# RMSNorm and matrix product: TensorE's program as a loop of sixteen tiles, and one store in 126 and 2 rows

## Chip, cores, metric

The kernel runs on one core of a Trainium2 chip. The metric is the device time of one execution in microseconds (us). A profiled execution also leaves a trace; its span runs from the first to the last instruction of the program, and all moments below are counted from the span's start.

A core has five engines, each with its own instruction stream: TensorE (PE; its weight loads are PEld), VectorE (DVE), ScalarE (ACT), GpSimd (POOL) and SyncE (SP). They meet only at semaphores. Sixteen DMA engines move data between the main memory and the on-chip memory; in this kernel nearly all transfers are issued by SyncE.

## The reference

```python
batch, seq, dim, out_dim = 16, 1024, 512, 768
def reference(x, gamma, weight, eps):
    rms = np.sqrt(np.mean(x ** 2, axis=-1, keepdims=True) + eps)
    x_norm = x / rms * gamma
    return np.matmul(x_norm, weight).astype(np.float32)
```

Inputs and output are float32. Seen as rows, x is 16384 x 512 and the output 16384 x 768.

## The kernel before

**Tiles.** The rows are cut into `NT` = 128 tiles of 128 rows; two tiles make a pair j (`NP` = 64). gamma is multiplied into the weights once, and the weights are kept as bfloat16 (`w_bf`, four blocks of 128 features). The division by the root mean square is left to the end: it scales each row of the product.

**Stages of a tile.** SyncE loads x, mostly sixteen or eight tiles at a time, into one of two buffers `xt`. GpSimd casts it to bfloat16 (`cast`, into `xb`). TensorE turns 128 x 128 blocks of 32-bit words, which hold two bfloat16 each (`transpose_word`, into the PSUM banks `tp`), and VectorE copies them out (`evac`, into `xT`). For the last four tiles of every sixteen, from tile 28 on, the turning is done by VectorE itself, in sixteen small moves (`cast_quad`, `move`, from `xq` into `xTq`; there are two buffers `xTq`). ScalarE squares and sums x for the norms (`square`, `root`), VectorE takes the reciprocal. Then TensorE does four steps of a weight load (`hold`) and two products, 512 and 256 columns wide (`matmuls`), into one of three accumulators `ops`; they are taken in turn, so that tile i uses the one of tile i-3. `finish_tile` scales the product into `ot`: ScalarE for even tiles, VectorE for odd ones. When a group of tiles is complete, SyncE stores it (`store`): eight tiles a store in the middle, at the end stores of 4, 4, 4, 2 and 2 tiles.

**Order.** Nothing is scheduled by a planner. The loop over j at the end of the kernel writes down every operation with the cells that it reads and writes (`order.add`), and `Order.emit` works out which semaphores each must wait for and issues all of them, unrolled, engine by engine in the order written. The transposes for pair j+2 are woven between the products of pair j by `feeder`. Each engine has one semaphore that counts up over the whole program (`done`), and an operation waits for a value of it. The last copy of a group waits for the copy before it (`before` in `finish_tile`), so that the store waits for one engine alone. SyncE's queue is in order: a store that waits holds back the loads behind it. The last store stands apart, after the final waits of the others.

Of the kernel before, what the change touches and what calls it, by code (L numbers as in the profile page):

```python
# [11 lines left out]
F32 = mybir.dt.float32  # L12
BF16 = mybir.dt.bfloat16
# [7 lines left out]
class Order:  # L21
# [1 line left out]

    def __init__(self, tc):  # L30
        self.tc, self.ops = tc, []

    def add(self, proc, engine, issue, reads=(), writes=()):
        self.ops.append((proc, engine, issue, list(reads), list(writes)))

    def transfer(self, engine, issue, reads=(), writes=()):
# [1 line left out]

    def emit(self):
        nc = self.tc.nc  # L40
        streams = {id(e): n for n, e in enumerate((nc.tensor, nc.vector, nc.scalar, nc.gpsimd, nc.sync))}
        writer, readers = {}, {}
        known = [dict() for _ in streams]
        clocks, needs, place, slot_of, slots = [], [], [], {}, []
        count = [0] * len(streams)
        for n, (proc, engine, _, reads, writes) in enumerate(self.ops):
            at = streams[id(engine)]
            if proc is None:
                me, turn = ("transfer", n), 1
            else:  # L50
                count[at] += 1
                me, turn = at, count[at]
            written = {writer[cell] for cell in reads + writes if cell in writer}
            read = {d for cell in writes for d in readers.get(cell, ())}
            need = []
            for d in sorted(written | read, reverse=True):
                who, when = place[d]
                if who == me and (engine is nc.tensor or d not in written):
                    continue
                if known[at].get(who, 0) < when:  # L60
                    need.append(d)
                    for k, v in clocks[d].items():
                        known[at][k] = max(known[at].get(k, 0), v)
            if proc is None:
                free = [k for k, d in enumerate(slots) if known[at].get(("transfer", d), 0)]
                if free:
                    slots[free[0]] = n
                else:
                    slots.append(n)
                slot_of[n] = ("slot", slots.index(n))  # L70
            clock = dict(known[at])
            clock[me] = turn
            place.append((me, turn))
            clocks.append(clock)
            needs.append(need)
            for cell in reads:
                readers.setdefault(cell, []).append(n)
            for cell in writes:
                writer[cell], readers[cell] = n, []
        awaited = {d for need in needs for d in need}  # L80
        seen = {who for clock in known for who in clock}
        last = [n for n, (me, _) in enumerate(place) if me not in seen and not isinstance(me, int)]
        sems, marks, done = {}, {}, {}
        for n in range(len(self.ops)):
            me = slot_of.get(n, place[n][0])
            if n in slot_of or n in awaited:
                if me not in sems:
                    sems[me] = self.tc.alloc_semaphore(f"done{len(sems)}")
                done[me] = done.get(me, 0) + (16 if n in slot_of else 1)
                marks[n] = (sems[me], done[me])  # L90
        for n, (proc, engine, issue, _, _) in enumerate(self.ops[:-1]):
            for d in needs[n]:
                engine.wait_ge(*marks[d])  # L93
            ins = issue()
            if n in marks:
                ins.then_inc(marks[n][0], 16 if n in slot_of else 1)
        return [marks[n] for n in last if n < len(self.ops) - 1], self.ops[-1][2]


@with_exitstack  # L100
def kernel(
# [9 lines left out]
    PE, DVE, ACT, POOL, SP = nc.tensor, nc.vector, nc.scalar, nc.gpsimd, nc.sync  # L111
    order = Order(tc)

    def run(engine, issue, reads=(), writes=()):
        order.add(1, engine, issue, reads, writes)

    x = x.flatten_outer_dims()
    out = out.flatten_outer_dims()
# [37 lines left out]
    jk = [sb(f"jk{n}", [P, D], BF16) for n in range(2)]  # L156
    xT = [sb(f"xT{n}", [P, 2, 2, P, 2], BF16) for n in range(4)]
    xq = [sb(f"xq{n}", [P, 4, D], BF16) for n in range(2)]
    xTq = [sb(f"xTq{n}", [P, 4, 2, P, 2], BF16) for n in range(2)]
    ot = [sb(f"ot{n}", [P, OG, O], F32) for n in range(3)]  # L160
    ssq = sb("ssq", [P, NT], F32)
    rms = sb("rms", [P, NT], F32)
    rstd = sb("rstd", [P, NT], F32)
# [70 lines left out]
    def evac(j, t=0, n=2):  # L234
        b = bank(j, t)
        src = tp[b].rearrange("p t h m -> p t (h m)").bitcast(BF16)
        dst = xT[j % 4].rearrange("p t h m c -> p t (h m c)")
        run(DVE, lambda: DVE.tensor_copy(out=dst[:, t:t + n, :], in_=src[:, t:t + n, :]),  # L238
            [("tp", b)], cells("xT", j % 4, t, n))
        for a in range(t, t + n):  # L240
            xT_of[2 * j + a] = (xT[j % 4][:, a], ("xT", j % 4, a))

    def transpose_tile(i):
        for h in range(2):
# [11 lines left out]
    def cast_quad(q):  # L256
        src, of = x_of(4 * q, 4)
        s = 4 * q // XG % 2
        run(POOL, lambda: POOL.tensor_copy(out=xq[s], in_=src), of, [("xq", s)])  # L259
        for t in range(4):  # L260
            xT_of[4 * q + t] = (xTq[s][:, t], ("xTq", s))
        words = xq[s].rearrange("p t d -> p (t d)").bitcast(F32).rearrange("p (a w) -> p a w", w=P)
        turned = xTq[s].rearrange("p t h m c -> p (t h m c)").bitcast(F32).rearrange("p (a m) -> p a m", m=P)
        for tokens in range(0, P, B):
            for features in range(0, P, B):
                quad_moves.append((turned[features:features + B, :, tokens:tokens + B],
                                   words[tokens:tokens + B, :, features:features + B], s))

    def move(dst, src, s):
        run(DVE, lambda: DVE.transpose(out=dst, in_=src), [("xq", s)], [("xTq", s)])  # L270

    def move_quad(n):
        for _ in range(min(n, len(quad_moves))):
# [5 lines left out]
        else:  # L279
            run(DVE, lambda: DVE.tensor_single_scalar(out=dst, in_=src, scalar=r, op=mybir.AluOpType.mult), reads, writes)  # L280

    turns = iter(range(NT + 1))

    def accumulator():
        return next(turns) % 3

    def store(i):
        first, n = o_first[i], o_size[i]
        s = first // OG % 3
        if i == first + n - 1:  # L290
            src = ot[s][:, first % OG:first % OG + n, :]
            order.transfer(SP, lambda: SP.dma_start(out=rows(out, first, n), in_=src), reads=cells("ot", s, first % OG, n))  # L292

    def hold(lhsT, cell):
        run(PE, lambda: PE.ldweights(lhsT), [cell])  # L295
# [1 line left out]
    def product(dst, lhsT, rhs, start, stop, reads, writes):  # L297

        run(PE, lambda: PE.add_instruction(mybir.InstMatmult(  # L299
            name=nc.get_next_instruction_name(), engine=mybir.EngineType.PE,  # L300
            ins=[PE.lower_ap(rhs), PE.lower_ap(lhsT)], outs=[PE.lower_ap(dst)],
            start_tensor_calc=start, stop_tensor_calc=stop, tile_size=(P, P), tile_position=(0, 0), ldweights=False)),
            reads, writes)

    def matmuls(i, a, ks, feed=None):
        block, cell = xT_of[i]
        for k in ks:
            lhsT = block[:, k // 2, :, k % 2]
# [4 lines left out]
            if feed:  # L313
                feed()

    def finish_tile(i, a, engine):
        s = i // OG % 3

        before = [("ot", s, i % OG - 1)] if i == o_first[i] + o_size[i] - 1 else []
        scale(engine, ot[s][:, i % OG, :], ops[a][:, :O], rstd[:, i:i + 1],  # L320
              [("ops", a, 0), ("ops", a, 1), ("rstd", i)] + before, [("ot", s, i % OG)])
        store(i)

    def feeder(pairs, gaps, alone=False):
        queue = [(j, t, h) for j in pairs for t in range(2) for h in range(2)]
# [17 lines left out]
    def load_weights(h):  # L343
# [10 lines left out]
    run(POOL, lambda: POOL.memset(ident_f, 0.0), [], ["ident"])  # L354
    run(POOL, lambda: POOL.affine_select(out=ident_f, in_=ident_f, compare_op=mybir.AluOpType.not_equal, fill=1.0, base=0,
                                         pattern=[[-1, P]], channel_multiplier=1), ["ident"], ["ident"])
    spare = accumulator()

    def warm_up(n):
        hold(warm[:, :P], "warm")  # L360
        for _ in range(n):
            product(ops[spare][:, :WIDE], warm[:, :P], warm, True, True, ["warm"], [("ops", spare, 0)])

    def weights(k, engine, lo=0, hi=O):
        halves = [half for half in range(2) if lo <= half * WIDE < hi]
# [19 lines left out]
    weights(0, DVE, 0, WIDE)  # L385
    weights(0, DVE, WIDE, O)
    weights(1, ACT)
    acc = [accumulator() for _ in range(2)]
    for i in range(2):
        matmuls(i, acc[i], [0, 1])  # L390
    weights(2, DVE)
    weights(3, ACT)
    norms(2, 2)
    cast(4, 2)
    matmuls(0, acc[0], [2, 3])
    finish_tile(0, acc[0], ACT)
    matmuls(1, acc[1], [2, 3], feeder([1], [2, 2], alone=True))
    finish_tile(1, acc[1], DVE)
    cast(6, 2)


# [2 lines left out]
    for j in range(1, NP):  # L404
# [15 lines left out]
        if j < 3:  # L420
            feed = feeder([j + 1], mid if j == 1 else one, alone=j == 1)
        elif j == 3:
            feed = feeder([4, 5], both)
        elif j + 2 < NP and quad_of(j + 2) is None:
            feed = feeder([j + 2], two)
        else:
            feed = None
        for i, engine in ((2 * j, ACT), (2 * j + 1, DVE)):
            a = accumulator()
            matmuls(i, a, range(K), feed)  # L430
            finish_tile(i, a, engine)


    with tc.tile_critical():  # L434
# [45 lines left out]
```

## Time and profile before

| | |
|---|---|
| Time, median of 3 runs | 209.25 us (208.79, 209.25, 209.55) |
| Profiled execution, span | 207.5 us |
| Instructions | 2761 |
| PE busy | 193.3 us, 93% of the span (1212 instructions) |
| PEld busy | 72.6 us, 35% (717) |
| DVE busy | 149.3 us, 72% (255) |
| ACT busy | 144.5 us, 70% (343) |
| POOL busy | 59.8 us, 29% (34) |
| DMA | 85.62 MB, mean 413 GB/s; the data queue q1 takes 97.3% of 16 engines' span |
| Instruction fetches | q8: 7 packets, 0.11 MB; q14: 5 packets, 0.04 MB |

How to read it: a busy time is the time in which the engine had an instruction in work, and an engine that is busy for most of the span need not be what sets its end. In the page's line of slices the span is cut into 40 equal parts, and a digit is the busy share of one part in tenths. "Idle before" is the time for which an engine had nothing to do before an instruction, and the name behind the arrow is what ended it. A queue q in the DMA list is a ring of transfers: q1 carries the data, q8 and q14 carry instructions for the engines, and q10 the load of gamma. A packet is one piece of a transfer moved by one DMA engine.

### The profile page before, as it was taken

How to read it: one execution, taken by the hardware profiler on the slowest of the kernel's cores; microseconds unless marked ns; L12 is line 12 of the kernel's file. 1: busy time of each engine (PE TensorE's matmuls, PEld its weight loads, DVE VectorE, ACT ScalarE, POOL GpSimd, SP SyncE). 2: the span in 40 equal slices, each digit the busy share in tenths (PEclk: the TensorE clock that was granted, in tenths of full speed). 3: DMA queues.
4: the chain of work that ended last, by engine and by line, in shares of the span. 5: the costliest groups of instructions: out<-in, count | busy, mean ns of one | idle time of the engine just before them, and what ended most of it. 6: DMA issues, size and time to landing. Idle time of an engine off the chain costs nothing.

```text
span 207.5 us, 2761 instructions
## 1 busy us (share of the span) xinstructions
PE 193.3 (93%) x1212; PEld 72.6 (35%) x717; DVE 149.3 (72%) x255; ACT 144.5 (70%) x343; POOL 59.8 (29%) x34
## 2 busy tenths in 40 slices
PE   7779999999999999998999999999999999999940
PEld 1233434433443334342333333443334334433210
DVE  0446556999579966999379984999579984999530
ACT  4698897868777596763977877687867787683310
POOL 2156733009400291003900570006700175000000
PEclk9999999999999999999999999999999999999996
DMA  6999999999999999999999999999999999998993
GB/s 225 403 441 436 388 405 456 455 388 422 436 445 442 395 425 448 429 411 431 434 407 436 437 428 434 418 428 437 417 426 426 433 442 425 426 436 381 407 404 139
DMA packets 5632, 85.62 MB, mean 413 GB/s; under 512 B 626, under 2 KB 628, under 8 KB 1780
## 3 DMA queue, kind: packets, MB, share of 16 engines
q1 hardware_dynamic: 5616, 85.46, 97.3%
q8 instruction: 7, 0.11, 0.2%
q14 instruction: 5, 0.04, 0.0%
q10 hardware_dynamic: 4, 0.00, 0.0%
HBM read 35.13 MB, written 50.33 MB: 412 GB/s over the span
## 4 chain that ended last, share of the span: by engine, by line
PE 71%; DMA 16%; DVE 5%; issue 2%; SPq 1%; ACT 1%; POOL 1%; ACTq 0%
PE ps L299 62%; DMA xt<-in_x_dram 16%; PE ps L229 8%; DVE ot L280 2%; DVE xTq L270 2%; DVE xT L238 1%; SPq L344 1%; POOL xb L187 1%; ACT jk L195 0%; SPq L176 0%; ACT ot L278 0%; SPq L292 0%; DVE rstd L202 0%; SPq L475 0%; ACTq L93 0%
## 5 line engine op out<-in xcount | busy, mean ns | idle before, releaser
L299 PE MATMUL ps<-w_bf,xT 128*128 128x256 bf16 (+1 forms) x783 | 145.0, 325 | 3.4 <-ACT ot L278 1.3
L278 ACT ACTIVATE ot<-ps,rstd 128x768 f32<-128x768 f32 x64 | 57.4, 898 | 42.4 <-PE ps L299 40.5
L195 ACT ACTIVATE jk<-xt 128x512 bf16<-128x512 f32 x128 | 78.8, 619 | 8.3 <-DMA xt<-in_x_dram 8.2
L187 POOL CAST xb<-xt 128x2048 bf16<-128x2048 f32 (+3 forms) x21 | 46.3, 2218 | 113.2 <-DMA xt<-in_x_dram 111.4
L280 DVE TENSOR_SCALAR ot<-ps,rstd 128x768 f32<-128x768 f32 x64 | 64.8, 1013 | 9.9 <-PE ps L299 9.2
L295 PEld LDWEIGHTS <-xT 128*128 128x128 bf16 x400 | 39.3, 98 | 61.2 <-issue 53.2
L229 PE MATMUL ps<-ident_f,xb 128*128 128x128 f32 x200 | 54.4, 277 | 0.9 <-POOL xb L187 0.9
L238 DVE COPY xT<-ps 128x1024 bf16<-128x1024 bf16 (+1 forms) x53 | 34.5, 653 | 24.5 <-PE ps L229 22.8
L270 DVE STREAM_TRANSPOSE xTq<-xq 32x256 f32<-32x256 f32 x112 | 48.7, 435 | 3.4
L229 PEld LDWEIGHTS ps<-ident_f,xb 128*128 128x128 f32 x200 | 28.3, 143 | 46.5 <-issue 42.9
L299 PE MATMUL ps<-w_bf,xTq 128*128 128x256 bf16 (+1 forms) x217 | 41.8, 324 | 0.4
L195 ACT ACTIVATION_READ_ACCUMULATOR jk<-xt 128x1 f32 x128 | 24.3, 190 | 0.0
L295 PEld LDWEIGHTS <-xTq 128*128 128x128 bf16 x112 | 11.0, 98 | 14.5 <-issue 14.5
L259 POOL CAST xq<-xt 128x2048 bf16<-128x2048 f32 x7 | 13.3, 1893 | 0.0
L202 DVE RECIPROCAL rstd<-rms 128x8 f32<-128x8 f32 (+3 forms) x20 | 3.8, 192 | 7.9 <-ACT rms L200 7.7
L200 ACT ACTIVATE rms<-ssq,eps_sb 128x8 f32<-128x8 f32 (+3 forms) x20 | 6.0, 300 | 0.6
L299 PE MATMUL ps<-warm 128*128 128x512 bf16 x10 | 4.4, 582 | 1.4 <-DVE eps_sb L353 1.4
L278 ACT ACTIVATE w_bf<-w_f,g_sb 128x768 bf16<-128x768 f32 x2 | 1.9, 936 | 1.7 <-DMA w_f<-in_weight_dram 1.7
L376 DVE COPY g_sb<-ps 128x4 f32<-128x4 f32 x1 | 0.2, 163 | 3.2 <-PE ps L370 3.2
L340 ACT ACT_TABLE_LOAD x1 | 1.3, 1283 | 1.5 <-SPq L434 1.5
L280 DVE TENSOR_SCALAR w_bf<-w_f,g_sb 128x512 bf16<-128x512 f32 (+2 forms) x3 | 1.4, 481 | 1.1 <-DMA w_f<-in_weight_dram 1.1
L370 PEld LDWEIGHTS ps<-ident_f,g_row 2*128 2x128 f32 x2 | 0.3, 200 | 2.6 <-issue 2.6
(10 smaller groups left out, 2.0 us busy)
## 6 DMA issues: line engine op xcount, KB each, us to landing
out_dram<-ot SPq DMA_DIRECT2D x13, 3072.0 KB, 16.6
xt<-in_x_dram SPq DMA_DIRECT2D x9, 2048.0 KB, 21.1
xt<-in_x_dram SPq DMA_DIRECT2D x3, 4096.0 KB, 22.2
out_dram<-ot SPq DMA_DIRECT2D x4, 1536.0 KB, 11.3
out_dram<-ot SPq DMA_DIRECT2D x3, 768.0 KB, 7.0
w_f<-in_weight_dram SPq DMA_DIRECT2D x2, 768.0 KB, 5.8
xt<-in_x_dram SPq DMA_DIRECT2D x2, 512.0 KB, 5.2
xt<-in_x_dram SPq DMA_DIRECT2D x1, 1024.0 KB, 9.0
```

What stands on the lines that cost most here:

```text
L187: run(POOL, lambda: POOL.tensor_copy(out=xb[s][:, i % 8:i % 8 + n, :], in_=src), of, cells("xb", s, i % 8, n))
L195: run(ACT, lambda: ACT.activation(out=jk[j], in_=src[:, 0, :], func=AF.Square, accum_out=ssq[:, i:i + 1]), of, [("jk", j), ("ssq", i)])
L200: run(ACT, lambda: ACT.activation(out=rms[:, s], in_=ssq[:, s], func=AF.Sqrt, scale=1.0 / D, bias=eps_sb), [("ssq", t) for t in range(i, i ...
L202: run(DVE, lambda: DVE.reciprocal(out=rstd[:, s], in_=rms[:, s]), [("rms", i)], [("rstd", t) for t in range(i, i + n)])
L229: run(PE, lambda: PE.transpose(out=tp[b][:, t, h, :], in_=words[:, lo:lo + P], identity=ident_f), cells("xb", s, j % 4 * 2 + t) + ["ident" ...
L238: run(DVE, lambda: DVE.tensor_copy(out=dst[:, t:t + n, :], in_=src[:, t:t + n, :]), [("tp", b)], cells("xT", j % 4, t, n))
L259: run(POOL, lambda: POOL.tensor_copy(out=xq[s], in_=src), of, [("xq", s)])
L270: run(DVE, lambda: DVE.transpose(out=dst, in_=src), [("xq", s)], [("xTq", s)])
L278: run(ACT, lambda: ACT.mul(out=dst, in_=src, mul=r), reads, writes)
L280: run(DVE, lambda: DVE.tensor_single_scalar(out=dst, in_=src, scalar=r, op=mybir.AluOpType.mult), reads, writes)
L295: run(PE, lambda: PE.ldweights(lhsT), [cell])
L299: run(PE, lambda: PE.add_instruction(mybir.InstMatmult(name=nc.get_next_instruction_name(), engine=mybir.EngineType.PE, ins=[PE.lower_ap(r ...
```

## The change

TensorE's operations for the pairs 6 to 61 (tiles 12 to 123) are no longer issued one by one. `Order.add` notes for each of them its turn (eight pairs, sixteen tiles) and half-turn, and `emit` issues one turn's operations inside a hardware loop on TensorE that runs seven times, its head aligned to a block of instructions. What comes before stays ahead of the loop, and tiles 124 to 127 stay behind it. The other engines' streams stay unrolled.

For the loop each turn must be the same. So the accumulator of a tile follows from its place among sixteen (`accumulator(i)`), there is one buffer `xTq`, which pairs 6 and 7 use too, and the loop has semaphores of its own, one for each engine and half-turn (`own`). VectorE, ScalarE and GpSimd count them up when they finish an operation that the loop waits for, and a later product of the loop takes the whole count off again. Such an operation no longer counts up the engine's common semaphore; whoever else waits for it waits for the engine's next operation that does (`shared`). For that, ScalarE gets a small write to `told` after the last but one tile of a store, and VectorE's copy of the last tile waits for it.

The store of tiles 124 and 125 is issued as two transfers, of 126 rows and of 2.

```diff
     def add(self, proc, engine, issue, reads=(), writes=()):
+        if self.turn is not None and engine is self.tc.nc.tensor:
+            self.body.setdefault(self.turn, []).append((len(self.ops), self.half))
         self.ops.append((proc, engine, issue, list(reads), list(writes)))
...
                 if who == me and (engine is nc.tensor or d not in written):
                     continue
+                if n in spot:
+                    direct.setdefault(n, {}).setdefault(who, d)
...
-        awaited = {d for need in needs for d in need}
+        turns = sorted(self.body)
+        size = len(self.body[turns[0]])
...
+        waits = [sorted({place[d][0] for t in turns for d in needs[self.body[t][q][0]]}) for q in range(size)]
...
+        def shared(d):
+            if d not in events:
+                return d
+            return next(e for e in order[place[d][0]] if e > d and e not in events)
...
+        for (who, half), sem in own.items():
+            final = max(q for q, w in values if w == who and self.body[turns[0]][q][1] == half)
+            q = next(q for q in range(final + 1, size) if q not in flags and q not in taken and self.ops[self.body[turns[0]][q][0]][0] == "product")
+            taken[q] = (sem, -counts[who, half])
+
+        def give(n):
+            _, engine, issue, _, _ = self.ops[n]
             for d in needs[n]:
-                engine.wait_ge(*marks[d])
+                engine.wait_ge(*marks[shared(d)])
             ins = issue()
             if n in marks:
                 ins.then_inc(marks[n][0], 16 if n in slot_of else 1)
+            elif n in events:
+                ins.then_inc(own[place[n][0], events[n][1]], 1)
+
+        behind = max(spot)
+        late = [n for n in outer if n > behind and self.ops[n][1] is nc.tensor]
+        for n in outer:
+            if n < len(self.ops) - 1 and n not in late:
+                give(n)
+        with nc.Fori(0, len(turns), engines=[mybir.EngineType.PE], head_slot={mybir.EngineType.PE: 0}):
+            for q, (n, half) in enumerate(self.body[turns[0]]):
+                for who in waits[q]:
+                    nc.tensor.wait_ge(own[who, half], values[q, who])
+                ins = self.ops[n][2]()
+                if n in marks:
+                    ins.then_inc(marks[n][0], 1)
+                elif q in taken:
+                    ins.then_inc(*taken[q])
+        for n in late:
+            give(n)
...
-    xTq = [sb(f"xTq{n}", [P, 4, 2, P, 2], BF16) for n in range(2)]
+    xTq = sb("xTq", [P, 4, 2, P, 2], BF16)
     ot = [sb(f"ot{n}", [P, OG, O], F32) for n in range(3)]
+    told = sb("told", [P, 1], F32)
...
+        if j in (6, 7):
+            block, to = xTq[:, 2 * (j - 6):2 * (j - 5)], ["xTq"] * 2
+        else:
+            block, to = xT[j % 4], cells("xT", j % 4, 0, 2)
...
-    turns = iter(range(NT + 1))
-
-    def accumulator():
-        return next(turns) % 3
+    def accumulator(i):
+        return (2, 0, 1, 2, 0, 1, 0, 2, 0, 1, 2, 0, 1, 2, 0, 1)[(i - 12) % 16] if i >= 12 else (i + 2) % 3
...
-            order.transfer(SP, lambda: SP.dma_start(out=rows(out, first, n), in_=src), reads=cells("ot", s, first % OG, n))
+            for lo, hi in ((0, P - 2), (P - 2, P)) if first == NT - 4 else ((0, P),):
+                part = rows(out, first, n)[lo:hi], src[lo:hi]
+                order.transfer(SP, lambda part=part: SP.dma_start(out=part[0], in_=part[1]), reads=cells("ot", s, first % OG, n))
...
-        before = [("ot", s, i % OG - 1)] if i == o_first[i] + o_size[i] - 1 else []
+        ends = i == o_first[i] + o_size[i] - 1 and i > o_first[i]
+        before = [("told", i - 1)] if ends else []
...
         store(i)
+        if engine is ACT and i + 1 == o_first[i] + o_size[i] - 1:
+            run(ACT, lambda: ACT.mul(out=told, in_=eps_sb, mul=1.0), ["eps"], ["told", ("told", i)])
...
+        order.turn, order.half = ((j - 6) // 8, (j - 6) % 8 // 4) if 6 <= j < NP - 2 else (None, 0)
```

## The prediction

> **What bounds the kernel now.** I read the page's slices first, then busy time by stretch, then the chain of waits, and last the records of single DMA packets, which the trace keeps. The page:
>
> ```profile
> PE   7779999999999999998999999999999999999940
> PEclk9999999999999999999999999999999999999996
> DMA  6999999999999999999999999999999999998993
> ...
> q8 instruction: 7, 0.11, 0.2%
> ```
>
> TensorE and the 16 DMA engines are both full from the third slice to the last but two. Busy time cut at the same point of three sixteen-tile turns, then the rest (stretch, length, PE, PEld, DVE, ACT, POOL, clock, DMA share, GB/s):
>
> ```profile
> 118.35:141.77 23.42, 23.26 (x151) 8.88 (x88) 19.07 (x33) 17.57 (x43) 6.46 (x4) 1.00 1.00 427
> 141.77:165.19 23.42, 23.26 (x151) 8.88 (x88) 19.07 (x33) 17.32 (x42) 6.12 (x3) 1.00 1.00 427
> 165.19:188.61 23.42, 23.26 (x151) 8.88 (x88) 19.07 (x33) 17.57 (x42) 7.33 (x3) 1.00 1.00 429
> 188.61:199.38 10.77, 10.67 (x66) 3.13 (x32) 6.78 (x11) 3.60 (x4) 0.00 (x0) 1.00 0.93 395
> 199.38:207.54 8.16, 0.00 (x0) 0.00 (x0) 1.01 (x1) 0.00 (x0) 0.00 (x0) 0.79 0.57 235
> ```
>
> A turn takes 23.42 us each time, with TensorE busy 23.26 of it: no gap can be taken from TensorE there, and any gap put in is added. But what ends last is not TensorE (199.3 us). The tail by microsecond:
>
> ```profile
> 202.00:203.00 1.00, 0.00 (x0) 0.00 (x0) 0.00 (x0) 0.00 (x0) 0.00 (x0) 1.00 0.99 412
> 203.00:204.00 1.00, 0.00 (x0) 0.00 (x0) 0.00 (x0) 0.00 (x0) 0.00 (x0) 1.00 0.71 289
> 204.00:205.00 1.00, 0.00 (x0) 0.00 (x0) 0.00 (x0) 0.00 (x0) 0.00 (x0) 0.58 0.24 98
> 205.00:206.00 1.00, 0.00 (x0) 0.00 (x0) 0.00 (x0) 0.00 (x0) 0.00 (x0) 0.50 0.12 49
> ```
>
> The reader is to see the share fall in steps: 0.24 of 16 engines is about four, 0.12 about two. The packet records say it exactly. Each transfer ends with one 4-byte completion on each engine; those of the last store come at 203.60 to 203.93 us on ten engines, at 204.06, 204.44, 205.01, 205.54, 205.59 on five, and at 206.29 on the last. So one engine ends 2.7 us behind the pack, and the span closes 1.24 us after it (207.54). Followed back, packet by packet, the late engine is never idle, while the pack waits for stores between 190 and 200 us (about 2 us in all).
>
> One stall of TensorE is also caused by late loads; ScalarE waited for x, and TensorE for ScalarE:
>
> ```profile
> 96.83 0.63 ACT L195 ACTIVATE jk<-xt 128x512 bf16<-128x512 f32 x1 [3.59 <-DMA xt<-in_x_dram]
> ...
> 98.07 0.88 ACT L278 ACTIVATE ot<-ps,rstd 128x768 f32<-128x768 f32 x1
> 99.00 1.46 PE L299 MATMUL ps<-w_bf,xT 128*128 128x512 bf16 x8 [1.28 <-ACT ot L278]
> ```
>
> **The fetches.** TensorE's 1741 instructions become 449, of which 216 are the body, turned seven times for tiles 12 to 123. Before, q8 makes seven fetches of 16,384 bytes, 23 to 27 us apart. Their packets take 0.89 to 0.98 us, and six times the data packet right behind takes 1.28 to 1.40 us where such a packet has a median of 0.91: about 1.3 us of one engine's time for a fetch. The front, the body (aligned to 256 instructions) and the rest fill three blocks, so I take one fetch to stay and six to go: 6 x 1.3 / 16 = 0.49 us less for an engine on average. By phase the fetches at 50 and 76 us fell on different engines, so they don't pile up. For the latest engine the bounds are 0 (its packets show no fetch after 43 us) and 1.3 (the one at 27 us looks to be its own). I take the mean share, 0.49, since which engine is latest varies.
>
> **The split store.** Tiles 124 and 125 went out as 8 packets of 6,144 bytes on each engine, 0.234 us a packet (1.87 us). The 2-row load of gamma shows what two rows do: q10 has four packets, two of data and two completions, so two engines. 126 rows show nowhere. Bounds: spread like 128 rows, at most 8 an engine, no change; or all on one engine, 126 x 0.234 = 29.5 us. The largest number up to 16 that divides 126 is 14; nearest to the 16 by 8 of the rows seen, I take 14 engines with 9 rows (2.11 us, +0.23), two with none (-1.87), and two with a tenth row (+0.47). If the latest engine is one of the relieved, it ends at 204.4, and the next, 205.59 + 0.23 = 205.82, sets the end: -0.47. If not, +0.23 or +0.47. I take the first. [...]
>
> [...]
>
> **The back edge.** Nothing in the trace is a branch of TensorE. Sequencer records of four engines at the start show compare-and-branch rows of 33 to 47 ns, with the next instruction 0.15 to 0.29 us after their start. Bounds for each of six edges: 0, and a whole fetch, 0.91 for the packet in front plus 0.98 = 1.9 us. I take 0, because work is queued: the body's last wait is for ScalarE's copy of the tile three before. In the turn that ends at tile 91 that copy ran from 143.44 to 144.34 us; the copy of tile 90 began at 146.03, so with tile 91 (4 x 0.325 us) TensorE was supplied until 147.3, 2.9 us later. If that cover is gone: 6 x 0.29 = 1.7 us. Even that is not on the path that ends last, for the pack may slip 2.7 us before it passes the late engine.
>
> [...]
>
> **Accumulators.** Three stay, but two of every sixteen tiles (16m+2 and 16m+4) now wait for the tile two before, not three. ScalarE copies that one in 0.90 us, starting when its tile ends; the tile between, with two transposes, takes 4 x 0.325 + 2 x 0.109 = 1.52. Margin 0.6 us. ScalarE sat 0.92 us idle before each of these copies; late copies (72.6, 98.1) are of tiles 40 and 56, which keep distance three. Cost 0; without the cover up to 14 x 0.9 = 12.6 us.
>
> **The rest.** ScalarE gains 20 tiny writes to `told`, one for each store of more than one tile; the nearest row is the root:
>
> ```profile
> L200 ACT ACTIVATE rms<-ssq,eps_sb 128x2 f32<-128x2 f32 x5 | 1.5, 296 | 0.2
> ```
>
> 0.30 us, inside that 0.92 of idle time; behind it only squares are queued. VectorE's copy of a group's last tile now waits for it; for tile 127 that is 198.97 + 0.30 = 199.27 against a start at 199.38. Cost 0, at most 0.1. Fifteen stores now wait for VectorE's next move (0.44 us) after the copy, and with them the loads behind on SyncE's queue; the DMA share of 0.99 to 1.00 there means a backlog hides it; bare, 15 x 0.44 = 6.6 us. SyncE issues one DMA more (0.33 us, after 197.8), free before the last issue at 200.69. One `xTq` instead of two: the moves follow the copy of tile 16m+15 on VectorE anyway, 0.
>
> **The sum.** -0.49 (fetches) -0.47 (split store) + 0 + 0 = -0.96 us on the profiled execution of 207.54: 206.6. The median of the runs, 209.25, lies 1.7 above that execution, which I carry along: 208.3.
>
> **Rivals.**
> 1. The late engine is neither relieved nor freed of a fetch: 209.25 + 0.23 = 209.5. For it: its chain shows no later fetch, and 14 of 16 engines get more. Against: the delays recur at large loads on few engines.
> 2. All lateness goes: the end is the pack's with ten rows, 203.60 + 0.47 = 204.07 against 206.29, -2.2: 207.0. For it: the six late engines hold all the loss. Against: loads were slow without any fetch.
> 3. Slower: each back edge refetches its block and TensorE's queue doesn't cover it. 6 x 1.9 = 11.4, less the 2.7 of slack: +8.7, 218. It decides from 0.45 us an edge (2.7 / 6). For: nothing in the trace shows how deep that queue is. Against: the 2.9 us and the one-block body.
> 4. 126 rows on few engines, or one uncovered wait above: 210 and more.
>
> **How the numbers follow.** Forecast 0.50, its own range 207.7 to 208.8; rival 1 0.17, rival 2 0.10, rival 3 0.14, rival 4 0.09. Under about 0.3% (0.63 us) a measurement of this kernel can't tell a change from none. Faster: 0.43 of the forecast and rival 2, 0.53; same: 0.07 and rival 1, 0.24; slower: rivals 3 and 4, 0.23. The range: 206.9 holds rival 2, 210.0 rival 1 with its +0.47 and some bare waits; the far rivals stay out.
>
> **What would show it.** q8 with one or two packets; TensorE at 23.42 us a turn with no idle time at the edge; the last microseconds of the DMA shares steeper, the last completion near 205.3; the store of 126 rows in nine packets an engine on 14 engines. Wrong, if turns grow, if instruction packets stay at seven, or if the last engine still ends 2.5 us behind the pack.

## The result, and the profile after

The changed kernel takes 211.28 us (median of 4 runs, 210.84 to 211.93), the kernel before beside it 209.4 us (4 runs, 208.79 to 210.05). The ratio is 1.0105, with a 95% interval of 1.0082 to 1.0127: slower by about 2 us, where 208.3 us was forecast and 210.0 was the upper end of the range.

The profiled execution took 210.84 us; its page (span, slices, DMA queues):

```profile
span 209.0 us, 2823 instructions
...
PE   7789999999999999998999999999999999999900
PEclk9999999999999999999999999999999999999995
DMA  6999999999999899999999999999999999999991
...
q8 instruction: 3, 0.05, 0.1%
```

TensorE's line now ends in two zeros where it ended in 4 and 0: TensorE is done earlier (198.7 us in the trace, 199.3 before), and the span is 1.5 us longer all the same. Three turns of the loop and the rest, cut at the back edges (stretch, length, then busy time of PE, PEld, DVE, ACT and POOL, clock, DMA share, GB/s):

```profile
120.36:143.78 23.42, 23.42 (x153) 8.88 (x88) 19.08 (x33) 17.75 (x45) 6.75 (x3) 1.00 1.00 427
143.78:167.20 23.42, 23.42 (x153) 8.88 (x88) 19.08 (x33) 17.76 (x45) 6.47 (x4) 1.00 1.01 431
167.20:190.62 23.42, 23.42 (x153) 8.88 (x88) 19.07 (x33) 16.45 (x41) 5.17 (x3) 1.00 1.00 427
190.62:198.72 8.10, 8.10 (x50) 2.35 (x24) 4.28 (x6) 2.98 (x6) 0.00 (x0) 1.00 0.95 395
```

A turn has its 23.42 us, with no idle time left in it. The loop's own rows on TensorE's sequencer (shortest, median, longest in ns):

```profile
L152 PEldq COMPARE_BRANCH  x8: 76/208/3425, 24.8 to 190.7; - x8
L152 PEldq ALU_OP  x7: 36/36/42, 49.4 to 190.6; - x7
```

Six back edges take 0.21 to 0.24 us each and the last, not taken, 0.08; all lie beside queued products. Only the entry at 24.8 us is long, 3.4 us; behind it TensorE's products have one gap of 0.46 us, which waits for VectorE's copy into `xTq` (the same program without a loop has that gap too, as is shown further down). The time went to the end (slices of 1 us, columns as above):

```profile
200.00:201.00 1.00, 0.00 (x0) 0.00 (x0) 0.00 (x0) 0.00 (x0) 0.00 (x0) 1.00 0.92 338
201.00:202.00 1.00, 0.00 (x0) 0.00 (x0) 0.00 (x0) 0.00 (x0) 0.00 (x0) 1.00 1.04 381
202.00:203.00 1.00, 0.00 (x0) 0.00 (x0) 0.00 (x0) 0.00 (x0) 0.00 (x0) 1.00 0.95 375
...
204.00:205.00 1.00, 0.00 (x0) 0.00 (x0) 0.00 (x0) 0.00 (x0) 0.00 (x0) 0.50 0.29 104
205.00:206.00 1.00, 0.00 (x0) 0.00 (x0) 0.00 (x0) 0.00 (x0) 0.00 (x0) 0.50 0.20 80
206.00:207.00 1.00, 0.00 (x0) 0.00 (x0) 0.00 (x0) 0.00 (x0) 0.00 (x0) 0.50 0.19 80
207.00:208.00 1.00, 0.00 (x0) 0.00 (x0) 0.00 (x0) 0.00 (x0) 0.00 (x0) 0.50 0.07 31
```

Two things are to be seen. Three engines (0.19 of 16) still work at 206 to 207 us, where before only one worked a third of that microsecond. And from 200 us on the engines are as busy as ever but move less: 0.95 of their time gives 375 GB/s at 202 us, where 0.99 gave 412 before. The packets are slow: from 150 us on the 6,144-byte packets of the two-tile stores took 234 ns each before, 269 at most; now 37 of 256 take over 300 ns, up to 854. The trace does not name the engine of a packet; but the packets listed below follow each other end to start within 0.01 us, so I read the last engine's back from the last completion (start in us, duration in ns):

```
split store:  202.90 241   203.14 340   203.48 494   203.98 624   204.60 234
              204.83 234   205.06 234   205.29 393   205.68 234   completion 205.91
last store:   eight packets of 234                                completion 207.76
```

Nine packets, four of them slow: 3.03 us, where eight of 234 ns are 1.87. Of the 1.16 us more, 0.23 is the ninth row and 0.92 the slow packets. Before, the last completion came at 206.29; the other 0.3 us stood already when the split store began (the store ahead of it was through at 202.90 us on this engine, at 202.59 on the latest one before).

### The profile page after: what moved, and what is told of

The parts are those of the page before. It is cut to its first block, busy times and chain, and to the rows that moved or that the text cites. A ratio compares the mean times of both kernels' runs of the same rounds, so it can differ in the third digit from the quotient of the medians.

```text
span 209.0 us, 2823 instructions
## 1 busy us (share of the span) xinstructions
PE 194.4 (93%) x1236; PEld 72.6 (35%) x717; DVE 149.4 (71%) x255; ACT 146.1 (70%) x363; POOL 59.8 (29%) x34
## 4 chain that ended last, share of the span: by engine, by line
PE 71%; DMA 15%; DVE 6%; issue 1%; SPq 1%; ACT 1%; POOL 1%; ACTq 0%
PE ps L369 62%; DMA xt<-in_x_dram 15%; PE ps L296 8%; DVE ot L350 2%; DVE xTq L340 2%; DVE xT L309 1%; POOL xb L254 1%; ACT jk L262 0%; SPq L418 0%; SPq L243 0%; ACT ot L348 0%; DVE xTq L309 0%; SPq L362 0%; DVE rstd L269 0%; SPq L546 0%
## 5 line engine op out<-in xcount | busy, mean ns | idle before, releaser
L369 PE MATMUL ps<-w_bf,xT 128*128 128x512 bf16 (+1 forms) x768 | 141.8, 326 | 1.5 <-DVE w_bf L350 0.8
L365 PEld LDWEIGHTS <-xT 128*128 128x128 bf16 x384 | 37.7, 98 | 58.3 <-issue 56.8
L369 PE MATMUL ps<-w_bf,xTq 128*128 128x512 bf16 (+1 forms) x256 | 49.0, 326 | 0.5 <-DVE xTq L309 0.5
L309 DVE COPY xT<-ps 128x1024 bf16<-128x1024 bf16 (+1 forms) x51 | 33.1, 652 | 22.2 <-PE ps L296 20.7
L365 PEld LDWEIGHTS <-xTq 128*128 128x128 bf16 x128 | 12.5, 98 | 17.1 <-issue 16.1
L396 ACT ACTIVATE told<-eps_sb 128x1 f32<-128x1 f32 x20 | 3.8, 192 | 0.0
L309 DVE COPY xTq<-ps 128x1024 bf16<-128x1024 bf16 x2 | 1.4, 692 | 2.4 <-PE ps L296 2.4
## 6 DMA issues: line engine op xcount, KB each, us to landing
out_dram<-ot SPq DMA_DIRECT2D x4, 1536.0 KB, 11.9
```

Of the source, the lines that this page charges most:

```text
L369: run(PE, lambda: PE.add_instruction(mybir.InstMatmult(name=nc.get_next_instruction_name(), engine=mybir.EngineType.PE, ins=[PE.lower_ap(r ...
```

## The experiments: the split store

All ratios are against the kernel before on the same chip; the brackets are 95% intervals. The first run took the split out of the changed kernel:

```diff
-            for lo, hi in ((0, P - 2), (P - 2, P)) if first == NT - 4 else ((0, P),):
-                part = rows(out, first, n)[lo:hi], src[lo:hi]
-                order.transfer(SP, lambda part=part: SP.dma_start(out=part[0], in_=part[1]), ...)
+            order.transfer(SP, lambda: SP.dma_start(out=rows(out, first, n), in_=src), ...)
```

> The changed kernel with the store of tiles 124 and 125 left whole (128 rows in one transfer). Theory S (the split store is what costs): the changed kernel's trace shows packets of 6,144 bytes taking 400 to 850 ns instead of 234 from 199.2 us on, when the split store runs; without the split they are gone and the time is that of the kernel before or less, ratio 0.993 to 1.002 (less by up to 0.5 us for the six fetches). Theory L (the loop with its accumulators, semaphores and later stores costs): the ratio stays at 1.008 to 1.013.

Measured: 209.76 us, 1.0044 [1.003, 1.0058], between the two theories. No 6,144-byte packet of the tail takes over 300 ns. The other half of the change, put into the kernel before:

```diff
-            order.transfer(SP, lambda: SP.dma_start(out=rows(out, first, n), in_=src), ...)
+            for lo, hi in ((0, P - 2), (P - 2, P)) if first == NT - 4 else ((0, P),):
+                part = rows(out, first, n)[lo:hi], src[lo:hi]
+                order.transfer(SP, lambda part=part: SP.dma_start(out=part[0], in_=part[1]), ...)
```

> The kernel before with only the store of tiles 124 and 125 in 126 and 2 rows. Theory S: nearly the whole loss, ratio 1.005 to 1.012, with slow packets of 6,144 bytes in the tail. Theory L: within 0.998 to 1.003. My prediction's step (the split relieves a late engine by 1.87 us) would give 0.997 to 0.998.

Measured: 210.62 us, 1.0089 [1.0067, 1.0112], with 29 packets over 300 ns. So both parts cost, and the split costs the more. Is it the tenth row, or something that any split brings? The next kernel has the two pieces as rows 0 to 111 and 112 to 127 (`P - 16` for `P - 2`):

> The kernel before with the same store in 112 and 16 rows: both numbers divide by 16, so each engine gets 7 and 1 rows, eight in all as before, but other rows than in a store of 128. If the split costs because engines get unequal numbers of rows (9, 10 and none), this is the kernel before, ratio 0.998 to 1.002. If it costs because engines then read rows that another engine reads elsewhere and packets slow down, the slow packets are here too and the ratio is 1.004 to 1.010. If the split costs nothing (theory L), 1.000.

Measured: 210.2 us, 1.0048 [1.003, 1.0065]. By its 640 completions (40 transfers of 16) both pieces use all sixteen engines, by division seven rows and one row on each, so eight as before, and yet 36 packets take over 300 ns, up to 1,025. Followed back, the engine that ended last (at 207.19 us) had seven rows and one, as many as before; its seven took 2.63 us in place of 1.64, two of them 532 and 901 ns. So slow packets cost by themselves, without an unequal share. Two kernels then kept the number of transfers, packets and packets an engine, and changed only which rows go out together; a third added a whole transfer:

```diff
+            for cut in (slice(0, P, 2), slice(1, P, 2)) if first == NT - 4 else (slice(0, P),):   # even and odd
+            for cut in (slice(0, P // 2), slice(P // 2, P)) if first == NT - 4 else (slice(0, P),):   # halves
...
-    o_first, o_size = stretches(OG, {0: [1, 1, 2, 4], last - 1: [4, 4], last: [4, 2, 2]})
+    o_first, o_size = stretches(OG, {0: [1, 1, 2, 4], last - 1: [4, 4], last: [2, 2, 2, 2]})
```

> The kernel before, with the store of tiles 124 and 125 cut into the 64 even rows and the 64 odd rows: four packets of 6,144 bytes on each engine twice, so eight an engine as before, and one transfer more. Theory P (a store whose rows no longer fall to the engines as 128 rows do makes two engines draw on the same rows' share of the memory, and both slow down): packets over 300 ns in the tail again, fewer than the 36 of 112 + 16 rows since the rows stay spread over all of the memory, ratio 1.002 to 1.006. Theory D (the price is that of one transfer more and its late issue): the same 1.005 as for 112 + 16. Theory U (only unequal row counts cost): no packet over 300 ns, ratio within 0.002 of 1.

> The kernel before, with the same store cut into rows 0 to 63 and rows 64 to 127: as many transfers, packets and packets an engine as with even and odd rows; only which rows go out together differs. Theory P: all 16 engines draw on one half of the memory at a time, so this is the worst of the splits: packets near 470 ns, twice the 234, summed excess over 234 ns well above the 10 us of 112 + 16, ratio 1.005 to 1.012. Theory D: the same as with even and odd rows and as 112 + 16, 1.005. Theory U: no slow packet, ratio 1.

> The kernel before, with the store of tiles 120 to 123 as two stores of two tiles (the last group 2, 2, 2, 2 in place of 4, 2, 2): one transfer more in the tail, but each of all 128 rows, in packets of 6,144 bytes. Theory P: no packet over 300 ns and ratio 1 to 1.002. Theory D: slow packets and about 1.005, as in every split so far.

Measured: even and odd rows 208.83 us, 0.9991 [0.9976, 1.0006], no packet over 300 ns; lower and upper half 209.14 us, 1.0008 [0.9993, 1.0023], 39 packets over 300 ns, 26 of the 39 between 390 and 530 ns, about twice the 234; one more whole transfer 209.06 us, 0.9996 [0.9985, 1.0006], none. The four microseconds from 199 us on, and the last three, in the kernel before and in three of these (columns as above). The kernel before:

```profile
199.00:203.00 4.00, 0.34 (x3) 0.00 (x0) 1.02 (x1) 0.00 (x0) 0.00 (x0) 1.00 0.97 402
```

Even and odd rows:

```profile
199.00:203.00 4.00, 0.00 (x0) 0.00 (x0) 0.34 (x1) 0.00 (x0) 0.00 (x0) 0.70 0.94 392
...
205.00:208.00 3.00, 0.00 (x0) 0.00 (x0) 0.00 (x0) 0.00 (x0) 0.00 (x0) 0.50 0.03 14
```

Lower and upper half:

```profile
199.00:203.00 4.00, 0.00 (x0) 0.00 (x0) 0.27 (x1) 0.00 (x0) 0.00 (x0) 0.99 0.98 336
...
205.00:208.00 3.00, 0.00 (x0) 0.00 (x0) 0.00 (x0) 0.00 (x0) 0.00 (x0) 0.50 0.03 10
```

126 + 2 rows alone:

```profile
199.00:203.00 4.00, 0.00 (x0) 0.00 (x0) 0.18 (x1) 0.00 (x0) 0.00 (x0) 0.84 0.94 344
...
205.00:208.00 3.00, 0.00 (x0) 0.00 (x0) 0.00 (x0) 0.00 (x0) 0.00 (x0) 0.50 0.08 33
```

Between 199 and 203 us both "half" and "126 + 2" fall to about 340 GB/s with the engines just as busy; even and odd rows stay at 392. So which rows a transfer holds decides whether packets slow down, and theory D falls. Theory P was right on the halves' packets and wrong on even and odd rows, where it expected slow ones and 1.002 to 1.006. Nor does P's price follow: the halves have the most slow packets (11.9 us over 234 ns summed, against 7.4 with 126 + 2) and cost nothing that can be measured. The latest engines show why. The halves' slow packets fell on engines with time to spare; the engine that ended last had none of them, its eight packets of the two halves took 234 ns each (202.06 to 203.92 us), and it was through at 205.77. With 126 + 2 one that was already late carried nine rows, three of them slow (406, 547 and 565 ns), and ended at 207.69. What counts is what the latest engine gets. These are readings of one traced execution each.

What these runs show is a dependence on the rows of a store: 39 slow packets with the halves, none with even and odd rows, at the same number of transfers and packets. Why 64 neighbouring rows are slower than every second row is not shown: no record of a packet says what the rows share, so the share of the memory in theory P stays a guess of mine.

The same 126 + 2 was then put on a store in the middle (`first == 64`, eight tiles, 24,576-byte packets):

> The kernel before, with 126 + 2 rows at the store of tiles 64 to 71 (packets of 24,576 bytes) and the tail whole. Theory P: slow packets at about 115 us, with four times the bytes of the tail's; the DMA engines have no idle time behind that to make it good, so the end comes 0.5 to 2 us later, ratio 1.003 to 1.010, with none over 300 ns among the 6,144-byte packets of the tail. Theory T (the price is a matter of the tail alone, where the last engine can't be caught up with): ratio within 0.002 of 1.

Measured: 214.54 us, 1.0262 [1.0243, 1.0282], 5.5 us, more than twice the upper end of what theory P gave; theory T falls. Stretches of 4 us around it:

```profile
120.00:124.00 4.00, 4.00 (x27) 1.35 (x14) 2.97 (x5) 3.12 (x10) 3.73 (x2) 1.00 1.00 430
124.00:128.00 4.00, 3.95 (x28) 1.68 (x17) 1.62 (x2) 3.09 (x7) 0.00 (x0) 1.00 1.00 397
128.00:132.00 4.00, 3.95 (x28) 1.55 (x16) 3.63 (x7) 3.08 (x9) 0.00 (x0) 1.00 1.03 379
132.00:136.00 4.00, 4.00 (x27) 1.60 (x16) 3.83 (x6) 2.55 (x8) 0.00 (x0) 1.00 1.02 350
```

The share stays at 1.00 and the rate falls to 350 GB/s, where the kernel before has, from 132 to 136 us:

```profile
132.00:136.00 4.00, 3.95 (x27) 1.58 (x16) 3.69 (x8) 3.08 (x9) 0.00 (x0) 1.00 1.00 428
```

Between 110 and 150 us 32 of the 24,576-byte packets take over 1,100 ns (median 912, one 3,567), where the kernel before has one; the loads beside them (16,384 bytes) have 14.4 us over their usual 611 ns in sum, instead of 4.1. Two engines, by this the ones without a row of the 126, ran ahead to no avail: the next load (issued at 120.3 us) had landed on them at 129.6 and 130.1 us, on the other fourteen only between 137.9 and 144.4; in the kernel before it landed on all sixteen between 136.2 and 140.4. There was no idle time to make it good, and TensorE, too, had to wait (1.3 us in all for this before, once):

```profile
PE ps L301 <- ACT ot L278: 3.6, 4, 2.1
```

Last, the changed kernel itself with even and odd rows in place of 126 + 2:

> The changed kernel with its second transfer kept but other rows: even and odd in place of 126 + 2. By theory P all of the split's price goes and that of the loop is left: 1.003 to 1.0045, against 1.0105. If the split costs beside a loop whatever its rows: 1.006 to 1.010.

Measured: 209.88 us, 1.0046 [1.0028, 1.0063], as with the loop and no split at all. The rows of that one store account for everything that the changed kernel loses beyond the loop: 0.6%, about 1.2 us, less than the 0.89% that the split costs alone.

## The experiments: the loop

The loop alone costs 0.4% although TensorE ends earlier. To take the loop away and keep all it needed:

```diff
-        with nc.Fori(0, len(turns), engines=[mybir.EngineType.PE], head_slot={mybir.EngineType.PE: 0}):
-            for q, (n, half) in enumerate(self.body[turns[0]]):
+        for t in turns:
+            for q, (n, half) in enumerate(self.body[t]):
```

> The changed kernel with the store whole and the loop written out: the same 112 tiles, waits and accumulators, but 1741 instructions of TensorE in a row, so seven instruction fetches again and no branch. The loop kernel alone measured 1.0044. Theory F (the loop costs: the stop of 2.4 to 3.4 us at its entry, or the fetch at 194 us in the tail where nothing can be made good): back to 1.000, within 0.002. Theory W (the stores' later waits, the accumulators or the told writes cost, and the loop is free): 1.0044 or, with seven fetches paid again, up to 1.007.

The second goes back to the class `Order` of the kernel before, so that stores wait for their own copies, and keeps accumulators, `told` and the one `xTq`; the third keeps the loop and adds, behind the copy that ends a group, `run(DVE, lambda: DVE.memset(sent, 0.0), [], ["sent"])` for the store to wait for:

> As the last one, but with the semaphores of the kernel before: each store waits for its own last copy and not for VectorE's next operation. What is left of the change are the accumulators at distance 2, the told writes and the one xTq. Theory W1 (fifteen stores 0.45 us later each): 1.000 within 0.002, and below the unrolled kernel by 0.004. Theory W2 (accumulators, told, xTq): 1.004 like the unrolled kernel. Theory F: 1.000, like the unrolled kernel.

> The changed kernel with the store whole, the loop kept, and a one-column write on VectorE right behind the copy that ends a group, for which the store then waits: so the store goes out some 0.1 us after its copy, not 0.45 us. Theory W1: 1.000 to 1.001. Theories F and W2: 1.004 as for the loop alone.

Measured: unrolled 209.22 us, 1.0008 [0.9988, 1.0028]; with the old semaphores 209.1 us, 0.9993 [0.9976, 1.001]; loop with prompt stores 209.65 us, 1.003 [1.0015, 1.0045]. Accumulators, `told` writes, the single buffer and the later stores cost nothing that these runs can see; a price is there only with the loop, though on this chip a small one (209.65 against 209.22 and 209.1 us). In the three loops up to here the packets of q8 come at about 25, 31 and 194 us, in these two unrolled kernels and the kernel before some 25 us apart, with none after 176. Two kernels moved them, by one turn written out ahead of the loop or behind it (`len(turns) - 1` in the loop):

> The loop alone, store whole, with six turns in the loop and the seventh written out behind it: the loop is left at 167 us, so the fetch behind it should come at about 170 us in place of 194 us, three fetches in all. Theory Ft (the loop's 0.3 to 0.4% is the fetch that falls into the last 14 us, on an engine that can't make it good): ratio 0.998 to 1.001. Theory Fe (it is the two fetches close together at the entry, 25 and 31 us): 1.003 to 1.005, as the loop alone. A third, that fewer fetches or the loop itself move the DMA's phases: also 1.003 to 1.005.

> The mirror of it: the first turn written out ahead, six turns in the loop, so the entry with its stop and its fetches moves from 25 to about 48 us and the fetch at 194 us stays. Theory Ft: 1.003 to 1.005, as the loop alone. Theory Fe: 0.998 to 1.002 if two close fetches hurt only in the first loads, else as the loop alone.

Measured: last turn out 209.75 us, 1.0028 [1.0013, 1.0043]; first turn out 209.83 us, 1.0033 [1.0016, 1.0049]. The first of them missed its purpose: it has a fetch at 172 us and one at 196 us as well. The second moved the entry's second fetch to 56 us and cost the same. That leaves Fe little, and Ft undecided. The next three put a late fetch where there was no loop (the first edit, on the unrolled kernel), and tried to take it away where there was one (the second edit, on the loop and, for comparison, on the unrolled kernel):

```diff
-    warm_up(6)
+    warm_up(4)
+    for _ in range(56):
+        product(ops[1][:, :8], warm[:, :P], warm[:, :8], True, True, ["warm"], [("ops", 1, 0)])
...
-            matmuls(i, range(K), feed)
+            matmuls(i, range(K) if i < NT - 4 else [0, K - 1], feed)
```

> The unrolled kernel (no loop, store whole) with two of the warm-up's first products replaced by 56 of eight columns: 54 more instructions of TensorE while it has nothing to do, so every instruction fetch should come some 6 us earlier and an eighth one fall at about 195 us. Theory Ft (a fetch in the last 14 us is what the loop costs): 1.003 to 1.004 like the loops, all of which have one at 194 to 196 us. Theory Lp (the loop itself costs, whatever the fetches): 1.000 to 1.001 like the unrolled kernel.

> The loop alone, store whole, but the last four tiles are computed from two of the four pieces of the features (24 instructions fewer behind the loop, so that what follows it ends inside the body's own 16 KB): the fetch at 194 us should be gone and two be left. TensorE ends some 2.6 us earlier. Theory Ft: no slower than the unrolled kernel with the same end. Theory Lp: slower than that by 0.003 to 0.004.

> The unrolled kernel with the same shortened end (the last four tiles from two of the four pieces): what the short end is worth by itself, for comparison. Both theories: seven fetches, the last at about 176 us; 0.995 to 1.001, since the late DMA engine sets the end and not TensorE.

Measured: unrolled with a fetch at 196 us 209.5 us, 1.0027 [1.0013, 1.004]; loop with the short end 209.49 us, 1.0028 [1.0014, 1.0042], the fetch at 195 us still there; unrolled with the short end 209.15 us, 1.001 [0.9996, 1.0023]. The first of the three spoke for the fetch: without a loop it is as slow as the loop with the short end on the same chip. Its page has one fetch more than the kernel before:

```profile
q8 instruction: 8, 0.13, 0.2%
```

Then the body was begun in the middle of a block (`head_slot` 128 in place of 0; a block here is what one fetch brings, 16,384 bytes, and between two fetches of the kernel before TensorE's trace has 237 to 267 instructions, 252 on average):

> The loop alone, store whole, with the body begun at the middle of a 16 KB block of instructions in place of its start: the body then lies in two blocks, and what follows it ends inside the second, with no boundary left to cross in the last 14 us. Theory A (both blocks stay held from turn to turn): no fetch at 194 us and, by theory Ft, 0.999 to 1.001. Theory B (each crossing inside the body brings in the block behind and the back edge brings the first one again): ten and more fetches, TensorE stops at each edge as at the entry (2.4 to 3.4 us), 1.05 to 1.12; this is also what the slower rival of the prediction would have cost.

Measured: 210.08 us, 1.0037 [1.0022, 1.0052].

```profile
span 208.9 us, 2821 instructions
...
q8 instruction: 2, 0.03, 0.1%
```

Two fetches, at 26 and 42 us, none later, and the body in two blocks turns without another one: theory B falls, and with it what the prediction's slower rival rested on. But the loop still costs its 0.4%. And its entry takes only 0.17 us here, where it takes 2.4 to 3.5 us in the other loops: the stop at the entry, the other half of theory F, is not the price either. The last run put the extra instructions in the middle of the unrolled program:

```diff
         for t in turns:
+            if t == turns[3]:
+                for _ in range(54):
+                    nc.tensor.ldweights(self.idle)
```

> The unrolled kernel (no loop, store whole) with 54 weight loads of 32 columns, whose weights nothing uses, put ahead of tile 60, where TensorE waits anyway at 98 us: start and the first fetches stay as they are, the later ones move some 6 us ahead, and an eighth falls at about 195 us. Theory Ft: 1.002 to 1.004, as with the instructions at the start. Theory St (what cost there was the early fetch at 19 us, in the first loads): 1.000 to 1.001. A delay of TensorE by 1 to 2 us behind 98 us comes with it; the late DMA engine never waits for TensorE, so by itself it should cost nothing.

Measured: 209.44 us, 1.0016 [1.0002, 1.003], with a fetch at 197 us: between the two expectations.

What follows for the loop: seven kernels with it lie at 1.0028 to 1.0046, three without it and without a late fetch at 0.9993 to 1.001, and two without it but with a late fetch at 1.0016 and 1.0027. On one and the same chip the loop is 0.3 to 0.6 us behind the unrolled kernel (209.65 against 209.22 and 209.1, 209.49 against 209.15) and level with the one that has a late fetch (209.49, 209.5). So a price goes with the loop; that the loop alone brings it is not shown. A fetch in the last microseconds is not its cause, or not alone: the loop in two blocks has none. Nor do the traces show the harm that theory Ft supposes. Nine traced executions have a fetch behind 190 us (seven loops, the changed kernel among them, and two unrolled kernels), and in none did the engine that ended last take it, followed back packet by packet. In the loop alone the engine that took it at 194.60 us (0.95 us, and 0.84 us in place of 0.46 for the data packet behind it) was through at 204.19 us, 2.1 us before the last, at 206.31. What the loop's 0.6 to 1.0 us are is not settled, and neither is why 54 more instructions cost the unrolled kernel 0.2 to 0.3%. One traced execution of each kernel does not show it: the latest engine's completion of the store that ends at about 184 us lies at 183.9 to 185.0 us in the loops, and at 184.1 to 184.8 in the unrolled kernels of this section and the kernel before.

## Why the prediction was wrong

**What bounds.** Right: the end hangs on the DMA engine that is latest, not on TensorE, which ended 0.6 us earlier to no avail. Of the sixteen completions that the text lists for the last store, the one at 204.44 is the late engine's completion of the store ahead of it; so five engines, not six, ended behind the pack.

**The split store, -0.47: the step that failed.** "I take 14 engines with 9 rows" fits: the 40 transfers leave 624 completions, 38 of 16, and 14 and 2 for the pieces. "If the latest engine is one of the relieved" was the choice, and it was the wrong one: no run shows the -0.47, and the engine that ended last in the changed kernel had nine rows. And a term was missing altogether. The sum priced each row at 234 ns, since that was all the trace showed; no row showed what a packet costs when the rows fall otherwise on the engines. The trace has it at 0.92 us on the latest engine, and the ninth row at 0.23; the runs have the term at +0.89% (about 1.9 us) alone and +0.6% (1.2 us) beside the loop, in place of -0.47 us. The test that the text named, "if the last engine still ends 2.5 us behind the pack", came out against it: the last store's completions now lie between 203.40 and 207.76 us, 4.4 us apart, where they lay 2.7 apart.

**The fetches, -0.49.** They went from seven to three, two more than the one that was to stay. The step that failed is spreading their 1.3 us over sixteen engines: the end is set by one engine, and for that one the text's own lower bound was 0. Unrolled, with seven fetches again, the kernel stood at 1.0008, 0.3% below the loop: no gain is to be seen, and the loop brought 0.6 to 1.0 us that stand in no term and whose cause stays open.

**The back edge, 0.** Right on TensorE: 0.21 to 0.24 us an edge, hidden, in turns of 23.42 us. The trace did hold one branch of TensorE, which the text says it does not: a compare-and-branch row at 0.82 us, of 0.17 us, nearer to the edges than the 33 to 47 ns of the other engines. The entry's 3.4 us had not been seen coming. It cost TensorE no gap: the 0.46 us behind it stand in the unrolled kernel as well, which has no entry:

```profile
PE ps L367 <- DVE xTq L309: 0.5, 1, 0.5
```

**Accumulators, `told`, one `xTq`, the stores' wait, 0.** Right within 0.2%: 0.9993 with the first three, 1.0008 with the wait as well. The one `xTq` does bring that gap on TensorE, which the kernel before does not have, but TensorE does not set the end. `told` takes 0.19 us where 0.30 was taken from the root's row:

```profile
L396 ACT ACTIVATE told<-eps_sb x20: 188/192/194, 14.6 to 198.3; 128x1 f32<-128x1 f32 x20
```

Fifteen stores do wait for VectorE's move, but the waits on VectorE's copies and moves have not grown: 162.3 us in 19 waits, where the kernel before has 164.0 in 19. After, then before:

```profile
SPq L362 <- DVE xTq L340: 152.5, 15, 12.3
SPq L362 <- DVE ot L350: 9.8, 4, 3.7
...
SPq L292 <- DVE ot L280: 95.1, 12, 12.2
SPq L292 <- DVE xTq L270: 68.9, 7, 10.9
```

**The rivals.** Rival 1 had the right engine, neither relieved nor freed, but without the slow packets and the loop's price only 209.5. Rival 2 and the forecast fell with the relief. Rival 3 fell: no refetch, not even with the body in two blocks. Rival 4 named the time, "210 and more", for another reason than few engines or a bare wait.

## What to carry to other kernels

Where the DMA engines are full (here a share of 1.00 in every turn), an edit is worth what it gives or takes on the engine that ends last; a saving spread over sixteen engines may be worth nothing (the loop alone, with three fetches in place of seven: 1.0044), and what is added on that engine counts whole (1.16 us more in its packets and 0.3 us of a later start, 1.5 us more span). Keep a transfer at all 128 rows, or cut it so that each piece still reaches over all of them (even and odd rows: 0.9991; 126 + 2: 1.0089; the halves' 1.0008 was luck, since their slow packets missed the engine that ended last); in the middle of a full queue the wrong cut cost 2.6%. When the DMA share stays at 1.00 and the GB/s fall (here to 350 from 428, at 132 to 136 us), look at the durations of single packets.

## What was not expected of the hardware

- With a store of all 128 rows, or of every second one, a 6,144-byte packet takes 234 ns and at most 272. With pieces of 64 neighbouring rows, of 112 + 16 or of 126 + 2, 29 to 39 of the 256 in the tail take over 300 ns, up to 1,032 (one trace each).
- SyncE's issue of the second piece takes longer than the usual 0.33 us, whether the packets are slow or not (0.99 us with even and odd rows, 1.18 with halves, 0.97 in the changed kernel). It does not delay the last store, which is issued 1.36 us after TensorE's last product as before:

```profile
L362 SPq DMA_DIRECT2D out_dram<-ot x23: 332/333/965, 11.9 to 200.1; - x23
```

- A loop whose body of 216 instructions began at slot 128 of a block of 16,384 bytes, and by 252 instructions a fetch reached into a second one, turned seven times with two fetches in all, at 26 and 42 us.
- Instructions added in idle time (54 of them) moved every later fetch ahead by 4 to 8 us and added one, at 196 or 197 us.
